# Row normalisation by the sum of absolute values: twelve-row tiles in four buffers, or sixteen-row tiles in three

## The chip, the cores and the metric

The kernel runs on one core of one Trainium2 chip. The metric is the device time of one execution in microseconds (us), the median of several runs. Before the change it is 316.64 us (three runs, 316.41 to 316.7).

## The reference

```python
batch, seq, dim = 32, 512, 1024
x = np.random.randn(batch, seq, dim).astype(np.float32)

def reference(x):
    sums = np.sum(np.abs(x), axis=-1, keepdims=True)
    return (x / (sums + 1e-8)).astype(np.float32)
```

There are 32 x 512 = 16,384 rows of 1,024 float32 values, 4 KB each. Every row is divided by the sum of its absolute values. The input is 67.1 MB and so is the output.

## The kernel before

The 16,384 rows are spread over the 128 partitions of the on-chip memory, 128 rows to a partition. A partition's rows of one tile lie side by side in DRAM, so that one partition of a tile is one run of consecutive bytes, up to 48 KB long.

There are eleven tiles: ten of 12 rows per partition (6 MB) and a last one of 8 (4 MB). The list `rows` holds these numbers. `piece` says where a tile lies in DRAM. Tiles 0, 1 and the last one share a block of 32 rows per partition (`HEAD`): their runs start 128 KB apart from partition to partition. Each of the other eight tiles is a block of its own, with runs 48 KB apart.

`load(i)` (L87) issues one transfer from DRAM into a buffer of the pool `sbuf`, which has four buffers of 12 rows (48 KB per partition each). It is issued on the queue of the SP engine. `max_dma_last_dim` limits the bytes that one DMA descriptor moves: tiles 0 and 1 are loaded in descriptors of 48 KB, the others in halves of 24 KB (16 KB for the last).

`normalize` does the arithmetic on a tile in place. On VectorE (DVE in the profile) it sums the absolute values of each row (L47), adds the small constant (L54) and takes the reciprocal (L56). Then it scales the rows, in up to three groups. The first `kv` rows are scaled by one multiplication with the broadcast reciprocals on VectorE (L58). The next `kt` rows are scaled one by one on VectorE (L65), and the rest one by one on ScalarE (ACT, L68). The table `split` gives the sizes of the last two groups for the first three tiles and the last two; the six tiles between them are scaled by L58 alone.

`store(i)` (L97) writes the tile back, on ACT's queue. Store 0 is cut into two transfers: three rows in descriptors of 4 KB, and nine rows in descriptors of 36 KB. The store of the last but two tiles is cut into two halves of six rows. The last two stores use 48 and 32 KB descriptors, the others 24 KB.

The order of work is written out by hand (`manual_schedule`). First come four loads. Then, for each tile: its arithmetic, its store, and the load of the tile four places further on, which reuses its buffer. That load therefore waits for this store to have landed. Each engine carries its instructions out in the order written; SP holds only loads, ACT holds its rows and all stores. The transfers of both queues are carried out by the same 16 DMA engines. A tile's 128 partitions are shared out evenly, eight to a DMA engine.

Of the kernel before, what the change touches and what calls it, by code (L numbers as in the profile page):

```python
# [1 line left out]

# [4 lines left out]

FP32 = mybir.dt.float32
EPS = 1e-8


@with_exitstack
def kernel(
    ctx: ExitStack,
    tc: tile.TileContext,
    x: bass.AP,
    out: bass.AP,
):
    nc = tc.nc
    P = nc.NUM_PARTITIONS  # L20

    x_flat = x.flatten_outer_dims()
    out_flat = out.flatten_outer_dims()
    n, d = x_flat.shape

    R = 12
    BUFS = 4
    HEAD = 32
    per_partition = n // P
    assert n % P == 0 and (per_partition - HEAD) % R == 0  # L30
    rows = [R] * ((per_partition - HEAD) // R + 2) + [HEAD - 2 * R]

    def piece(flat, i):
        head = flat[: P * HEAD, :].rearrange("(p r) d -> p r d", p=P)
        if i < 2:
            return head[:, R * i : R * (i + 1), :]
        if i == len(rows) - 1:
            return head[:, 2 * R :, :]
        a = P * (HEAD + R * (i - 2))
        return flat[a : a + P * R, :].rearrange("(p r) d -> p r d", p=P)  # L40

    sbuf = ctx.enter_context(tc.tile_pool(name="sbuf", bufs=BUFS))
    stats = ctx.enter_context(tc.tile_pool(name="stats", bufs=len(rows)))

    def normalize(x_tile, k, kv, kt):
        s = stats.tile([P, R], FP32)
        nc.vector.tensor_reduce(  # L47
            out=s[:, :k],
            in_=x_tile[:, :k, :],
            axis=mybir.AxisListType.X,  # L50
            op=mybir.AluOpType.add,
            apply_absolute_value=True,
        )
        nc.vector.tensor_scalar_add(out=s[:, :k], in0=s[:, :k], scalar1=EPS)  # L54
        inv = stats.tile([P, R], FP32)
        nc.vector.reciprocal(out=inv[:, :k], in_=s[:, :k])  # L56
        if kv:
            nc.vector.tensor_mul(  # L58
                out=x_tile[:, :kv, :],
                in0=x_tile[:, :kv, :],  # L60
                in1=inv[:, :kv].unsqueeze(2).to_broadcast([P, kv, d]),
            )
        for r in range(kv, kv + kt):
            row = x_tile[:, r, :]
            nc.vector.tensor_scalar_mul(out=row, in0=row, scalar1=inv[:, r : r + 1])  # L65
        for r in range(kv + kt, k):
            row = x_tile[:, r, :]
            nc.scalar.activation(  # L68
                out=row,
                in_=row,  # L70
                func=mybir.ActivationFunctionType.Copy,
                scale=inv[:, r : r + 1],
            )

    last = len(rows) - 1
    split = {0: (3, 4), 1: (0, 3), 2: (0, 3), last - 1: (0, 2), last: (4, 4)}

    tiles = {}

    HALF, WHOLE = 24576, 49152
    FIRST = 3

    def load(i):
        x_tile = tiles[i] = sbuf.tile([P, R, d], FP32, name="x_tile")
        nc.sync.dma_start(out=x_tile[:, : rows[i], :], in_=piece(x_flat, i), max_dma_last_dim=WHOLE if i < 2 else HALF)  # L87

    def store(i):
        if i == 0:  # L90
            parts = [(0, FIRST, 4 * d), (FIRST, R, WHOLE)]
        elif i == last - 2:
            parts = [(0, R // 2, HALF), (R // 2, R, HALF)]
        else:
            parts = [(0, rows[i], WHOLE if i >= last - 1 else HALF)]
        for a, b, size in parts:
            nc.scalar.dma_start(  # L97
                out=piece(out_flat, i)[:, a:b, :],
                in_=tiles[i][:, a:b, :],
                max_dma_last_dim=size,  # L100
            )

    def compute(i):
        k = rows[i]
        kt, ks = split.get(i, (0, 0))
        normalize(tiles[i], k, k - kt - ks, kt)

    with tc.manual_schedule():
        for i in range(BUFS):
            load(i)  # L110
        for i in range(len(rows)):
            compute(i)
            store(i)
            if i + BUFS < len(rows):
                load(i + BUFS)


# [1 line left out]
_INS = ['x']  # L119
_OUTS = [((32, 512, 1024), 'float32')]  # L120


# [23 lines left out]
```

## Time and profile before

The profiled execution has a span of 315.2 us; the median of the runs is 316.64 us.

| what | value |
|---|---|
| median of the runs | 316.64 us |
| span of the profiled execution | 315.2 us |
| first load issued, first reduce begins | 0.73, 17.80 us |
| last reduce begins, last store issued | 279.79, 293.25 us |
| VectorE busy | 260.6 us (83%) |
| of it L47, reduce (11 instructions) | 138.2 us |
| of it L58, multiply (10 instructions) | 113.6 us |
| of it L65, row by row (7 instructions) | 4.8 us |
| ACT busy | 18.5 us (6%) |
| L68, one row on ACT (16 instructions) | 1.138 us each |
| bytes moved, mean rate over the span | 134.22 MB, 426 GB/s |
| load of 6 MB, median from issue to landing | 36.9 us |

In the views of the profile, times are counted from the start of the span. q1 is the load queue (SP's), q10 the store queue (ACT's). In a view of windows the columns are: window, its length, busy time of VectorE, ACT and POOL with the number of instructions, the TensorE clock, the mean busy share of the 16 DMA engines, and GB/s. In a view of groups each line ends with busy time, mean length of one instruction in ns, and the idle time before them with what ended it. A packet is what a DMA engine carries out without a break; here, one descriptor.

### The profile page before, as it was taken

What the parts mean: (1) busy time and instruction counts of PE and PEld (TensorE: products, weight loads), DVE (VectorE), ACT (ScalarE), POOL (GpSimd) and SP (SyncE); (2) the same over time, 40 slices, a digit from 0 to 9 for tenths busy, and PEclk for the clock granted to TensorE, in tenths of its full rate; (3) what the DMA queues carried; (4) which work ended last, traced back from release to release, by engine and by line L of the source; (5) the groups of instructions that cost most, each with busy time, mean ns of one, the idle gap of its engine ahead of it and who ended that gap; (6) DMA issues with size and microseconds to landing.
All of it is one profiled execution on the core that took longest, in us unless ns stands there. A gap on an engine that the chain in (4) does not pass through costs nothing.

```text
span 315.2 us, 172 instructions
## 1 busy us (share of the span) xinstructions
DVE 260.6 (83%) x50; ACT 18.5 (6%) x17; POOL 0.2 (0%) x4
## 2 busy tenths in 40 slices
DVE  0079999999999999989996997999699969999000
ACT  0010503004000000000000000000000000203200
POOL 0000000000000000000000000000000000000000
DMA  8999999999999999999999999999999999999997
GB/s 318 480 399 412 437 407 464 411 436 413 415 446 437 415 446 437 415 449 434 415 449 437 412 449 437 412 449 437 415 446 437 415 437 434 432 428 496 399 408 324
DMA packets 5761, 134.22 MB, mean 426 GB/s; under 512 B 385, under 2 KB 385, under 8 KB 769
## 3 DMA queue, kind: packets, MB, share of 16 engines
q1 hardware_dynamic: 2736, 67.11, 49.8%
q10 hardware_dynamic: 3024, 67.11, 49.4%
q14 instruction: 1, 0.00, 0.0%
HBM read 67.11 MB, written 67.11 MB: 426 GB/s over the span
## 4 chain that ended last, share of the span: by engine, by line
DVE 40%; DMA 33%; another core or an unknown queue 18%; ACT 1%; issue 0%; SPq 0%
DVE s L47 23%; DMA x_tile<-in_x_dram 17%; DMA out_dram<-x_tile 16%; DVE x_tile L58 15%; ACT x_tile L68 1%; DVE x_tile L65 1%; DVE inv L56 0%; DVE s L54 0%; SPq L87 0%
## 5 line engine op out<-in xcount | busy, mean ns | idle before, releaser
L47 DVE TENSOR_REDUCE s<-x_tile 128x12 f32<-128x12288 f32 (+1 forms) x11 | 138.2, 12562 | 29.8 <-DMA x_tile<-in_x_dram 29.8
L58 DVE TENSOR_TENSOR x_tile<-x_tile,inv 128x12288 f32<-128x12288 f32 (+3 forms) x10 | 113.6, 11358 | 0.5
L68 ACT ACTIVATE x_tile<-x_tile,inv 128x1024 f32<-128x1024 f32 x16 | 17.2, 1138 | 256.9 <-DVE inv L56 256.9
L65 DVE TENSOR_SCALAR x_tile<-x_tile,inv 128x1024 f32<-128x1024 f32 x7 | 4.8, 749 | 0.0
L56 DVE RECIPROCAL inv<-s 128x12 f32<-128x12 f32 (+1 forms) x11 | 2.5, 226 | 0.4
L68 ACT ACT_TABLE_LOAD x1 | 1.3, 1283 | 17.8 <-DMA x_tile<-in_x_dram 17.8
L54 DVE TENSOR_SCALAR s<-s 128x12 f32<-128x12 f32 (+1 forms) x11 | 1.9, 174 | 0.4
L130 POOL MEMSET const-bfloat16-1.0<- 128x1 bf16 x1 | 0.1, 101 | 0.0
L130 POOL MEMSET const-uint8-127<- 128x1 uint8 x1 | 0.1, 101 | 0.0
L130 POOL MEMSET const-float32-0.0<- 128x1 f32 x1 | 0.1, 98 | 0.2 <-issue 0.2
L130 POOL MEMSET const-float32-1.0<- 128x1 f32 x1 | 0.1, 98 | 0.0
## 6 DMA issues: line engine op xcount, KB each, us to landing
x_tile<-in_x_dram SPq DMA_DIRECT2D x10, 6144.0 KB, 36.9
out_dram<-x_tile ACTq DMA_DIRECT2D x8, 6144.0 KB, 49.1
out_dram<-x_tile ACTq DMA_DIRECT2D x2, 3072.0 KB, 33.4
out_dram<-x_tile ACTq DMA_DIRECT2D x1, 4608.0 KB, 37.9
x_tile<-in_x_dram SPq DMA_DIRECT2D x1, 4096.0 KB, 32.2
out_dram<-x_tile ACTq DMA_DIRECT2D x1, 4096.0 KB, 20.9
out_dram<-x_tile ACTq DMA_DIRECT2D x1, 1536.0 KB, 29.3
```

Source lines behind the costliest of these rows:

```text
L47: nc.vector.tensor_reduce(out=s[:, :k], in_=x_tile[:, :k, :], axis=mybir.AxisListType.X, op=mybir.AluOpType.add, apply_absolute_value=True,)
L54: nc.vector.tensor_scalar_add(out=s[:, :k], in0=s[:, :k], scalar1=EPS)
L56: nc.vector.reciprocal(out=inv[:, :k], in_=s[:, :k])
L58: nc.vector.tensor_mul(out=x_tile[:, :kv, :], in0=x_tile[:, :kv, :], in1=inv[:, :kv].unsqueeze(2).to_broadcast([P, kv, d]),)
L65: nc.vector.tensor_scalar_mul(out=row, in0=row, scalar1=inv[:, r : r + 1])
L68: nc.scalar.activation(out=row, in_=row, func=mybir.ActivationFunctionType.Copy, scale=inv[:, r : r + 1],)
L130: nc = _bacc.Bacc("TRN2", target_bir_lowering=False, num_devices=1)
```

## The change

There are three buffers of 16 rows per partition in place of four of 12. The tiles are seven of 16 rows and two of 8 (`rows`), nine in all. They lie in three blocks (`pieces`): tiles 0 and 8 share 24 rows per partition, tiles 1 to 3 share 48, and tiles 4 to 7 share 56, so that the runs start 96, 192 and 224 KB apart.

`load` and `store` no longer limit the descriptors: one descriptor moves the whole run of a partition, 64 KB for a tile of 16 rows and 32 KB for a tile of 8. Each tile is stored by one transfer.

In `normalize` the multiplication with the broadcast reciprocals is gone. Every row is scaled by itself: the last three eighths of a tile's rows on ACT (6 of 16, 3 of 8), the others on VectorE (10 and 5). The reduce, the add and the reciprocal remain, on 16 or 8 rows. The table `split` and the cut stores go. The written order is as before, with three loads ahead, and with load i+3 after store i.

```diff
-    R = 12
-    BUFS = 4
-    HEAD = 32
-    per_partition = n // P
-    assert n % P == 0 and (per_partition - HEAD) % R == 0
-    rows = [R] * ((per_partition - HEAD) // R + 2) + [HEAD - 2 * R]
+    R = 16
+    BUFS = 3
+
+    pieces = [(0, 8), (1, 2, 3), (4, 5, 6, 7)]
+    rows = [16, 16, 16, 16, 16, 16, 16, 8, 8]
+    assert n == P * sum(rows)
+
+    place = {}
+    base = 0
+    for tiles_of in pieces:
+        per = sum(rows[i] for i in tiles_of)
+        at = 0
+        for i in tiles_of:
+            place[i] = (base, per, at)
+            at += rows[i]
+        base += P * per
 
     def piece(flat, i):
-        head = flat[: P * HEAD, :].rearrange("(p r) d -> p r d", p=P)
-        if i < 2:
-            return head[:, R * i : R * (i + 1), :]
-        if i == len(rows) - 1:
-            return head[:, 2 * R :, :]
-        a = P * (HEAD + R * (i - 2))
-        return flat[a : a + P * R, :].rearrange("(p r) d -> p r d", p=P)
+        start, per, at = place[i]
+        block = flat[start : start + P * per, :].rearrange("(p r) d -> p r d", p=P)
+        return block[:, at : at + rows[i], :]
...
-    def normalize(x_tile, k, kv, kt):
+    def normalize(x_tile, k, ks):
...
-        if kv:
-            nc.vector.tensor_mul(
-                out=x_tile[:, :kv, :],
-                in0=x_tile[:, :kv, :],
-                in1=inv[:, :kv].unsqueeze(2).to_broadcast([P, kv, d]),
-            )
-        for r in range(kv, kv + kt):
+        for r in range(k - ks):
             row = x_tile[:, r, :]
             nc.vector.tensor_scalar_mul(out=row, in0=row, scalar1=inv[:, r : r + 1])
-        for r in range(kv + kt, k):
+        for r in range(k - ks, k):
             row = x_tile[:, r, :]
             nc.scalar.activation(
...
-    split = {0: (3, 4), 1: (0, 3), 2: (0, 3), last - 1: (0, 2), last: (4, 4)}
...
-        nc.sync.dma_start(out=x_tile[:, : rows[i], :], in_=piece(x_flat, i), max_dma_last_dim=WHOLE if i < 2 else HALF)
+        nc.sync.dma_start(out=x_tile[:, : rows[i], :], in_=piece(x_flat, i))
 
     def store(i):
-        if i == 0:
-            parts = [(0, FIRST, 4 * d), (FIRST, R, WHOLE)]
-        elif i == last - 2:
-            parts = [(0, R // 2, HALF), (R // 2, R, HALF)]
-        else:
-            parts = [(0, rows[i], WHOLE if i >= last - 1 else HALF)]
-        for a, b, size in parts:
-            nc.scalar.dma_start(
-                out=piece(out_flat, i)[:, a:b, :],
-                in_=tiles[i][:, a:b, :],
-                max_dma_last_dim=size,
-            )
+        nc.scalar.dma_start(out=piece(out_flat, i), in_=tiles[i][:, : rows[i], :])
...
-            compute(i)
+            normalize(tiles[i], rows[i], 3 * rows[i] // 8)
             store(i)
             if i + BUFS < len(rows):
                 load(i + BUFS)
```

More of the change, by code (lines that the diff above doesn't have):

```diff
@@ L24 @@
     n, d = x_flat.shape
-    R = 12
-    BUFS = 4
-    HEAD = 32
-    per_partition = n // P
-    assert n % P == 0 and (per_partition - HEAD) % R == 0
-    rows = [R] * ((per_partition - HEAD) // R + 2) + [HEAD - 2 * R]
-    def piece(flat, i):
-        head = flat[: P * HEAD, :].rearrange("(p r) d -> p r d", p=P)
-        if i < 2:
-            return head[:, R * i : R * (i + 1), :]
-        if i == len(rows) - 1:
-            return head[:, 2 * R :, :]
-        a = P * (HEAD + R * (i - 2))
-        return flat[a : a + P * R, :].rearrange("(p r) d -> p r d", p=P)
+    R = 16
[12 more added lines that the diff above has]
+        base += P * per
+    def piece(flat, i):
+        start, per, at = place[i]
+        block = flat[start : start + P * per, :].rearrange("(p r) d -> p r d", p=P)
+        return block[:, at : at + rows[i], :]
     sbuf = ctx.enter_context(tc.tile_pool(name="sbuf", bufs=BUFS))
-    stats = ctx.enter_context(tc.tile_pool(name="stats", bufs=len(rows)))
-    def normalize(x_tile, k, kv, kt):
+    stats = ctx.enter_context(tc.tile_pool(name="stats", bufs=2 * len(rows)))
+    def normalize(x_tile, k, ks):
         s = stats.tile([P, R], FP32)
@@ L73, in normalize @@
             )
-    last = len(rows) - 1
-    split = {0: (3, 4), 1: (0, 3), 2: (0, 3), last - 1: (0, 2), last: (4, 4)}
     tiles = {}
-    HALF, WHOLE = 24576, 49152
-    FIRST = 3
     def load(i):
         x_tile = tiles[i] = sbuf.tile([P, R, d], FP32, name="x_tile")
-        nc.sync.dma_start(out=x_tile[:, : rows[i], :], in_=piece(x_flat, i), max_dma_last_dim=WHOLE if i < 2 else HALF)
+        nc.sync.dma_start(out=x_tile[:, : rows[i], :], in_=piece(x_flat, i))
     def store(i):
-        if i == 0:
-            parts = [(0, FIRST, 4 * d), (FIRST, R, WHOLE)]
-        elif i == last - 2:
-            parts = [(0, R // 2, HALF), (R // 2, R, HALF)]
-        else:
-            parts = [(0, rows[i], WHOLE if i >= last - 1 else HALF)]
-        for a, b, size in parts:
-            nc.scalar.dma_start(
-                out=piece(out_flat, i)[:, a:b, :],
-                in_=tiles[i][:, a:b, :],
-                max_dma_last_dim=size,
-            )
[L103 to L106, printed above, removed]
+        nc.scalar.dma_start(out=piece(out_flat, i), in_=tiles[i][:, : rows[i], :])
     with tc.manual_schedule():
```

## The prediction

> **What bounds the kernel now.** I read the page's slices and queues first, to see which resource has no gaps.
>
> ```profile
> span 315.2 us, 172 instructions
> ...
> DVE 260.6 (83%) x50; ACT 18.5 (6%) x17; POOL 0.2 (0%) x4
> ...
> DMA  8999999999999999999999999999999999999997
> ...
> DMA packets 5761, 134.22 MB, mean 426 GB/s; under 512 B 385, under 2 KB 385, under 8 KB 769
> ...
> q1 hardware_dynamic: 2736, 67.11, 49.8%
> q10 hardware_dynamic: 3024, 67.11, 49.4%
> ```
>
> The packets of the load queue (q1, issued by SP) and of the store queue (q10, issued by ACT) fill 49.8% + 49.4% = 99.2% of the 16 DMA engines' span: 312.7 of 315.2 us. Only the first and last slices are below 9 tenths. VectorE has 54.6 us to spare. So the kernel is bound by bytes, which don't change, and a new version can gain only what packets cost beside their bytes. It can lose any stretch in which both queues are empty.
>
> Next come the loads' waits, the windows, and the instructions by form.
>
> ```profile
> SPq L87 <- DMA out_dram<-x_tile: 242.1, 8, 63.3
> ```
> ```profile
> 12.00:14.00 2.00, 0.00 (x0) 0.00 (x0) 0.00 (x0) 1.00 0.91 393
> 292.00:294.00 2.00, 0.00 (x0) 1.22 (x2) 0.00 (x0) 1.00 0.91 393
> ```
> ```profile
> L47 DVE TENSOR_REDUCE s<-x_tile 128x12 f32<-128x12288 f32 x10 | 129.5, 12949 | 29.8 <-DMA x_tile<-in_x_dram 29.8
> ...
> L47 DVE TENSOR_REDUCE s<-x_tile 128x8 f32<-128x8192 f32 x1 | 8.7, 8686 | 0.0
> ```
> ```profile
> 0.73 247.25 SPq L87 DMA_DIRECT2D x_tile<-in_x_dram  x11
> 17.80 12.95 DVE L47 TENSOR_REDUCE s<-x_tile 128x12 f32<-128x12288 f32 x1 [17.80 <-DMA x_tile<-in_x_dram]
> ...
> 36.67 2.07 DVE L65 TENSOR_SCALAR x_tile<-x_tile,inv 128x1024 f32<-128x1024 f32 x3
> 36.78 2.40 ACTq L97 DMA_DIRECT2D out_dram<-x_tile  x2
> ...
> 288.96 4.27 ACT L68 ACTIVATE x_tile<-x_tile,inv 128x1024 f32<-128x1024 f32 x4 [17.82 <-DVE inv L56]
> 288.96 2.74 DVE L65 TENSOR_SCALAR x_tile<-x_tile,inv 128x1024 f32<-128x1024 f32 x4
> 293.25 0.34 ACTq L97 DMA_DIRECT2D out_dram<-x_tile  x1
> ```
>
> Every load past the fourth waits for a store to land, for its buffer. In each window shown 16 packets of 48 KB start, one per engine: 0.91 x 2.00 us = 1.82 us each. The last store is issued at 293.25, while the store before it still runs (issued 279.85, landed 304.5 by its semaphore), so the engines have work to the end.
>
> **Descriptors.** The trace's packet records give the spacing of packets on one engine: 1.812 us for 48 KB, 1.209 for 32 KB, 0.908 for 24 KB. The slope from 24 to 48 KB is 0.904 us / 24,576 B = 0.0368 ns per byte, which leaves 4 to 5 ns per packet. A 64 KB packet, of which the trace has none, is then an estimated 2.414 us; were its fixed part ten times larger it would be 2.45. Now each engine moves (5761 - 385) / 16 = 336 data packets; after it is 2 x (7 x 8 + 2 x 8) = 144. So 192 x 4.5 ns = **0.9 us less**. Beside it, load packets followed by a store packet are 6.5 ns longer than the rest on average (914.8 against 908.3 ns, 1,637 of them), nearly all of it between 39 and 65 us, where the 4 KB pieces of store 0 alternate with load packets: 0.66 us per engine. This can go with those pieces (0.66) or come back where stores first meet loads (0); I take 0.3, the middle.
>
> **Compute.** The reduce grows by (12.949 - 8.686) / 4 = 1.066 us a row: 17.2 us for 16 rows. The add and the reciprocal take 0.5 us (30.77 to 31.26). The multiply at L58 goes; its rows move to L65, at 2.07 / 3 to 2.74 / 4 = 0.69 us each on VectorE (10 of 16, 5 of 8), and to ACT at 4.27 / 4 = 1.07 us (6 and 3). So 17.2 + 0.5 + 6.9 = 24.6 us for a 16-row tile and 8.7 + 0.5 + 3.4 = 12.6 for an 8-row one; ACT's 6.4 and 3.2 run beside VectorE's. VectorE's sum falls to 7 x 24.6 + 2 x 12.6 = 197 us. This is worth **nothing** by itself: the transfers of a 16-row tile take 16 x 2.414 = 38.6 us and cover it. The nine loads and nine stores, for eleven and thirteen, cost no path time either, at about 0.4 us of queue time each, under running transfers. On ACT the store of a tile stands before the next tile's rows, which aren't due for another 17 us; on SP only loads stand behind a waiting load. POOL has no part in it.
>
> **First tile.** Load 0 now lands at 17.78 after eight packets, so 3.3 us are start. It will land at 3.3 + 8 x 2.414 = 22.6, and store 0 is issued at 47.3. Loads 1 and 2 keep the engines busy to 3.3 + 24 x 2.414 = 61.2. Cost 0.
>
> **Three buffers.** Load i+3 now waits for store i. Store 0 lands when 32 packets have gone, 3.3 + 32 x 2.414 = 80.5, and store 1 was issued some 9 us before, at about 71.7. In the middle each cycle has 38.6 us of transfers against 24.6 + about 2 for issue and landing, so about 12 us of cover: a store is always queued when the next load is issued. Cost 0 there; if the cover went, the missing time would be paid once a cycle.
>
> **The tail** decides. Load 8 waits for store 5. Before that the engines must do loads 0 to 6 and stores 0 to 5, 104 packets: 3.3 + 251.1 = 254.4; load 7's eight 32 KB packets alternate with store 5's, so it lands between 254.4 and 264.1. All but store 8 is done at 3.3 + 112 x 2.414 + 24 x 1.209 = 302.7. Store 8 is to be ready by then. It needs load 8 landed (0.4), 12.7 us of compute and 1.0 us from issue to first packet (load 0: issued 0.73, first packet 1.74), so load 8 must land by 289.0. If load 8 is issued at 264.1 and alternates one for one with all of store 6, it lands at about 264.1 + 1.0 + 8 x (2.414 + 1.209) = 294.1, less one packet if it goes first: 291.7. The engines then stand idle for 2.7 to 5.1 us. Each packet of store 6 that doesn't get in front takes off 2.4 us; two packets decide.
>
> What settles the order is how a new transfer gets in. In the trace a transfer that comes to busy engines starts late: store 0, issued at 36.78, has its first packet at 40.54, 3.75 us after; load 4, issued at 76.84, at 80.45, 3.6 after. That is 2.6 us more than on idle engines, and on most engines three 24 KB packets start in between. Read as packets already taken from the other queue, it is three of 64 KB, 7.2 us; read as time it stays 2.6 us, one packet. I take the count, because the 2.6 us are close to three packets in both places, though equal sizes can't prove it. Then the loads, newcomers in each cycle, fall behind the stores, so that store 5 lands at about 261, load 8 joins behind load 7 with no wait of its own, and store 6, issued at 262 to 267, is the newcomer. Load 8, with its first packet near 263, then has one to six store packets in between: it lands at 276 to 288.3 (263 + 9.7 + 0.4 and 2.4 for each). **Cost 0**; the bounds of the tail are 0 and 5.1 + 2.6 = 7.7 us.
>
> **Sum.** Span 315.2 - 0.9 - 0.3 = 314.0. The median of the runs is 316.64 - 315.16 = 1.5 above the profiled span, so **315.4 us**, a gain of 0.4%. The walk's own end, 302.7 + 8 x 1.209 + 0.4 + 1.0 = 313.8, agrees.
>
> **A rule that speaks against the change.** The trace's packets alternate one for one between the queues wherever both have work. The Trainium skill's page "DMA: Bandwidth & Descriptors", section "Queues, rings and completion order", says that an engine drains a whole packet of typically 9 to 17 descriptors from one queue before it switches. The rival on whole transfers below is worked out as a mechanism of this kernel.
>
> **The rivals.**
> - *The newcomer's delay is a time, and the tail starves.* Load 8 comes after 289 us, and the engines wait for store 8. For it: the delay is the same 3.6 to 3.75 us twice; the walk without a count of packets is 3 to 5 us too late. Against it: packets taken ahead explain the same rows. Price 2 to 7.7, say 4.4: 319.8 us, **slower**; it decides once load 8 lands after 289.
> - *Engines drain one queue's whole share of a transfer before they switch.* Store 6's eight packets go first, 264 to 283.3; load 8 ends at 293.0, lands at 293.4, store 8's first packet is at 307.1, 4.4 us late: 319.8. Against it: alternation by single packets in all mixed stretches of the trace.
> - *The large descriptor doesn't arrive as one packet but as two of 32 KB.* Then 256 packets per engine, 0.5 us of the 0.9 given back, and a newcomer's three packets are again small, 3.6 us: idle 0 to 2. 315.9 to 317.9, say 316.5.
> - *The new strides cost rate.* Partition runs now start 96, 192 and 224 KB apart, for 48 and 128 KB. Against it: 48 KB packets took 1.815 us at both old strides. 1% of the transfers is 3 us: 318.4.
>
> **How the numbers follow.** Chances: covered tail 45%, delay as a time 36%, two packets 9%, strides 6%, whole transfers 4%. A difference under 0.2%, 0.63 us, can't be told from none in this kernel. Of the covered tail I put 38 of 45 below 316.0, the rest within; two packets is 1 faster, 5 within, 3 slower; the delay as a time is 2 within and 34 slower; the other two are slower. Faster 39%, same 14%, slower 47%. The forecast's own range is 314.7 to 316.3. With the starved tail it reaches to 320.8, where the top of its bound and the far strides are left out.
>
> **What would show it.** Right: q1 and q10 together at 99% of a span near 314; packets of 64 KB at 2.41 us; all slices but the outer ones at 9; the last reduce starting by 289; VectorE busy near 197. Wrong: a gap in the DMA row in slices 38 to 40, the last reduce after 289, with the gap as long as the reduce is late; or packets well above 2.41 us; or 32 KB packets throughout. A gap in the middle of the span would show that three buffers fail in the cycle, which nothing above expects.

## The result, and the profile after

The changed kernel takes **328.82 us** (median of four runs, 327.32 to 330.79) against 316.56 for the kernel before on the same chips (316.41 to 316.7): a ratio of 1.0391, 95% interval 1.0352 to 1.0429. The profiled execution is the fastest of the four, 327.32 us, with a span of 325.54 us (315.16 before). So 10.4 of the 12.3 us are in the profile, whose run is 1.5 us faster than the median. About 0.15 us lie outside the span: 1.78 us here, for 1.63 in 47 later runs of the kernel before. A run more than 1.5% above the fastest of its kernel counts as slow and stays out of the medians and ranges below, which concerns one run of experiment 3 (321.85 us) and one of experiment 7 (330.01 us).

The page of the changed kernel, span, slices and queues:

```profile
span 325.5 us, 256 instructions
...
DVE 195.4 (60%) x107; ACT 52.2 (16%) x49; POOL 0.2 (0%) x4
...
DMA  9899898989999999998998999999999998989647
...
DMA packets 2594, 134.24 MB, mean 412 GB/s; under 512 B 288, under 2 KB 288, under 8 KB 288
...
q1 hardware_dynamic: 1296, 67.11, 48.4%
q10 hardware_dynamic: 1296, 67.11, 48.0%
```

The two queues fill 96.4% of the span, where they filled 99.2%: by the packet records 313.7 us of packets on each engine, for 312.9 before. The bytes take about as long as they did; what is new is time without packets. The DMA row shows where: a 6 and a 4 in the slices 38 and 39. VectorE's time fell by a quarter, and the kernel is slower all the same.

The same stretch in the view of windows (window, length, busy time of VectorE, ACT and POOL, clock, DMA share, GB/s), and in the timeline (start, length, engine, line):

```profile
264.00:266.00 2.00, 1.06 (x2) 0.64 (x1) 0.00 (x0) 1.00 0.19 82
...
306.00:308.00 2.00, 2.00 (x1) 0.00 (x0) 0.00 (x0) 1.00 0.12 49
308.00:314.00 6.00, 5.29 (x8) 3.23 (x3) 0.00 (x0) 1.00 0.00 0
```
```profile
240.53 17.22 DVE L53 TENSOR_REDUCE s<-x_tile 128x16 f32<-128x16384 f32 x1 [14.24 <-DMA x_tile<-in_x_dram]
...
265.15 0.34 ACTq L82 DMA_DIRECT2D out_dram<-x_tile  x1
267.83 8.69 DVE L53 TENSOR_REDUCE s<-x_tile 128x8 f32<-128x8192 f32 x1 [2.77 <-DMA x_tile<-in_x_dram]
...
280.54 0.34 ACTq L82 DMA_DIRECT2D out_dram<-x_tile  x1
300.83 8.69 DVE L53 TENSOR_REDUCE s<-x_tile 128x8 f32<-128x8192 f32 x1 [20.37 <-DMA x_tile<-in_x_dram]
...
313.54 0.34 ACTq L82 DMA_DIRECT2D out_dram<-x_tile  x1
```

The chain that ended last has store 5 and load 8 in these two pieces (start, length):

```profile
226.38 40.22 DMA out_dram<-x_tile
...
266.67 34.13 DMA x_tile<-in_x_dram
```

The last tile is reduced from 300.83, after VectorE has waited 20.37 us for load 8. Its store is issued at 313.54; the engines ran out of other work near 306.3. That is the large hole, 7.9 us by the packet records (16 engines' mean, 306.2 to 314.5). A small one of 1.2 us lies at 264.4 to 266.2: on 13 of the engines load 7 and store 5 are done, store 6 is only issued at 265.15, and load 8 waits until 266.67 for store 5 to land. Before there was no hole at all between the first packet and the last. 7.9 + 1.2 us of holes and 0.8 us more of packets are 9.9 of the 10.4 us; the rest lies at the start, at the end and in the few ns by which the record of one packet overlaps the next.

### The profile page after: what moved, and what is told of

Same layout as the page of the kernel before. It is cut to its first block, busy times and chain, and to the rows that moved or that the text cites. A ratio compares the mean times of both kernels' runs of the same rounds, so it can differ in the third digit from the quotient of the medians.

```text
span 325.5 us, 256 instructions
## 1 busy us (share of the span) xinstructions
DVE 195.4 (60%) x107; ACT 52.2 (16%) x49; POOL 0.2 (0%) x4
## 2 busy tenths in 40 slices
DMA packets 2594, 134.24 MB, mean 412 GB/s; under 512 B 288, under 2 KB 288, under 8 KB 288
## 4 chain that ended last, share of the span: by engine, by line
DMA 57%; DVE 26%; another core or an unknown queue 12%; issue 0%; DVEq 0%; SPq 0%; ACTq 0%
DMA x_tile<-in_x_dram 31%; DMA out_dram<-x_tile 27%; DVE s L53 19%; DVE x_tile L65 7%; DVE inv L62 0%; DVE s L60 0%; DVEq L117 0%; SPq L79 0%; DVEq L65 0%; ACTq L82 0%
## 5 line engine op out<-in xcount | busy, mean ns | idle before, releaser
L53 DVE TENSOR_REDUCE s<-x_tile 128x16 f32<-128x16384 f32 (+1 forms) x9 | 137.9, 15323 | 116.8 <-DMA x_tile<-in_x_dram 116.8
L68 ACT ACTIVATE x_tile<-x_tile,inv 128x1024 f32<-128x1024 f32 x48 | 50.9, 1137 | 238.2 <-DVE inv L62 238.2
L65 DVE TENSOR_SCALAR x_tile<-x_tile,inv 128x1024 f32<-128x1024 f32 x80 | 53.8, 749 | 0.7
L62 DVE RECIPROCAL inv<-s 128x16 f32<-128x16 f32 (+1 forms) x9 | 2.2, 242 | 0.3
L60 DVE TENSOR_SCALAR s<-s 128x16 f32<-128x16 f32 (+1 forms) x9 | 1.6, 174 | 0.3
```

Source lines behind the costliest of these rows:

```text
L53: nc.vector.tensor_reduce(out=s[:, :k], in_=x_tile[:, :k, :], axis=mybir.AxisListType.X, op=mybir.AluOpType.add, apply_absolute_value=True,)
L68: nc.scalar.activation(out=row, in_=row, func=mybir.ActivationFunctionType.Copy, scale=inv[:, r : r + 1],)
```

## The experiments

Each is compared with the kernel before, run beside it (316.58 or 316.59 us median in these sets). "A" to "D" in the expectations are the theories as they were put there.

**1 and 2. Descriptors of 32 and of 16 KB** in the changed kernel.

```diff
-        nc.sync.dma_start(out=x_tile[:, : rows[i], :], in_=piece(x_flat, i))
+        nc.sync.dma_start(out=x_tile[:, : rows[i], :], in_=piece(x_flat, i), max_dma_last_dim=32768)
...
-        nc.scalar.dma_start(out=piece(out_flat, i), in_=tiles[i][:, : rows[i], :])
+        nc.scalar.dma_start(out=piece(out_flat, i), in_=tiles[i][:, : rows[i], :], max_dma_last_dim=32768)
```

> The changed kernel with one thing undone: each run of a partition moves in descriptors of at most 32 KB (two per partition for 16 rows). Theory A, packet size: in the changed kernel a transfer's completion waits for one more packet of the other queue (last packet of load 3 ends at 121.0, its reduce begins at 123.8), engines fall a packet out of step, and a newcomer waits for packet boundaries, all priced in packets of 2.42 us. With 1.21 us packets load 8 then lands by about 290 in place of 300.8, and the gap before the last store shrinks from 8 us to 0 to 2: 315.5 to 318 us. Theory B, three buffers: load 8 can't be issued before store 5 has landed near 265, whatever the packets; the gap stays at 6 to 8 us: 325 to 329. Theory C, strides: packets lose rate through the 96 to 224 KB strides; unchanged too, 327 to 329.

> The changed kernel with descriptors of at most 16 KB. Theory A: the three packet costs halve again, but 576 packets per engine at 4.8 ns cost 2 us more than 144 do: 316 to 318.5, gap near 0. Theory B: as the changed kernel, 325 to 331. Theory C: 327 to 331.

Measured: 320.77 us (320.1 to 321.17) and 321.32 us (320.6 to 321.83), ratios 1.0129 (1.0112 to 1.0146) and 1.0149 (1.013 to 1.0167). Both are 2.8 us above what theory A allowed and far below B and C. (With 16 KB there are 512 packets per engine, not 576; they take 315.7 us, 2 us more than the changed kernel's.) Page and timeline with 32 KB:

```profile
DMA  8999999999999999999999999999999997999997
```
```profile
266.40 8.68 DVE L53 TENSOR_REDUCE s<-x_tile 128x8 f32<-128x8192 f32 x1
266.58 0.38 ACTq L82 DMA_DIRECT2D out_dram<-x_tile  x1
...
287.97 8.69 DVE L53 TENSOR_REDUCE s<-x_tile 128x8 f32<-128x8192 f32 x1 [8.95 <-DMA x_tile<-in_x_dram]
300.69 0.35 ACTq L82 DMA_DIRECT2D out_dram<-x_tile  x1
```

The large hole is gone: the last reduce begins at 287.97, inside the prediction's limit of 289. The small one has stayed and grown, 2.4 us at 264.8 to 267.7 (the 7 in slice 34), so it doesn't come from the size of the packets alone. Besides it, packets are longer than their size asks by 3.2 us per engine, for 1.4 in the kernel before; 2.4 + 1.8 us are about what separates it from the kernel before, 4.2 us. With 16 KB the last reduce begins at 291.45 and the small hole is 1.7 us.

**3. The kernel before with 48 KB descriptors** in place of 24.

```diff
-    HALF, WHOLE = 24576, 49152
+    HALF, WHOLE = 49152, 49152
```

> The kernel before with all its 24 KB descriptors made 48 KB and nothing else. Theory A: each completion waits 1.8 us in place of 0.9, but four buffers and a tail of which the last load is issued near 247 leave slack: no gap, and 100 fewer packets per engine save 0.5 us: 316 to 317.5. If large packets cost by themselves (a stall per packet or a lower rate), 320 or more. Theory B: 316 to 316.6.

Measured: 318.65 us over nine runs, ratio 1.0046 (1.0021 to 1.007): 2 us slower, between the two ranges that were expected (316 to 317.5 and 320 or more). The runs scatter from 316.13 to 319.52, while those of the kernel before stay within 316.41 and 316.85 in all sets. The windows at the end of its profiled execution:

```profile
300.00:308.00 8.00, 0.00 (x0) 0.00 (x0) 0.00 (x0) 1.00 0.86 373
308.00:312.00 4.00, 0.00 (x0) 0.00 (x0) 0.00 (x0) 1.00 1.16 500
312.00:314.00 2.00, 0.00 (x0) 0.00 (x0) 0.00 (x0) 1.00 0.08 33
314.00:316.00 2.00, 0.00 (x0) 0.00 (x0) 0.00 (x0) 1.00 0.04 16
```

(Windows count a packet whole where it starts.) No hole, but the 16 engines don't end together: between 312.85 and the last packet a mean of 2.6 us is lost, for 0.3 us before. Here engines are a large packet or two out of step.

**4. A tail of 12 and 4 rows** in the changed kernel, with its 64 KB descriptors.

```diff
-    rows = [16, 16, 16, 16, 16, 16, 16, 8, 8]
+    rows = [16, 16, 16, 16, 16, 16, 16, 12, 4]
```

> The changed kernel with its last two tiles of 12 and 4 rows in place of 8 and 8; 64 KB descriptors and three buffers stay. If the loss is the gap in the tail (theories A and B alike), the last tile's own load and compute fall from 9.7 + 12.6 to 4.8 + 6.9 us and the store before it grows by 4.8: gap 0 to 2, 317 to 320 us. If the loss is rate or stalls spread over the span (theory C), 325 to 329.

Measured: 319.64 us (318.43 to 320.76), ratio 1.0097 (1.006 to 1.0133). Its DMA row has no hole, and both tiles of the tail come in time:

```profile
DMA  9999999999999999999999999999999999999995
```
```profile
273.81 12.95 DVE L53 TENSOR_REDUCE s<-x_tile 128x12 f32<-128x12288 f32 x1 [7.83 <-DMA x_tile<-in_x_dram]
292.80 0.34 ACTq L82 DMA_DIRECT2D out_dram<-x_tile  x1
296.40 4.42 DVE L53 TENSOR_REDUCE s<-x_tile 128x4 f32<-128x4096 f32 x1 [3.69 <-DMA x_tile<-in_x_dram]
303.50 0.34 ACTq L82 DMA_DIRECT2D out_dram<-x_tile  x1
```

So with everything else of the change in place, the shape of the tail alone is worth 9 us.

**5. Only store 6 in 32 KB descriptors.**

```diff
+        nc.scalar.dma_start(out=piece(out_flat, i), in_=tiles[i][:, : rows[i], :], max_dma_last_dim=32768 if i == 6 else 65536)
```

> The changed kernel; store 6 alone moves in two 32 KB descriptors per partition, all else in 64 KB. Theory D, turns: the queues take turns by packets, so load 8's eight 32 KB packets each wait for one 64 KB packet of store 6 (8 x 3.63 = 29 us), and that is what makes the last reduce late. With equal packets load 8 takes 8 x 2.42 = 19.4 us, the last reduce begins near 291 in place of 300.8, and the gap of 8 us falls to 0 to 1: 319 to 322 us. Theory A as first put (completions and steps between engines, in all transfers): those are unchanged but for one transfer, so the gap stays at 5 us or more: 325 or more.

Measured: 321.13 us (319.27 to 322.86), ratio 1.0143 (1.0088 to 1.0197). Page and timeline:

```profile
DMA  9999999999999999999999999999999999899997
```
```profile
268.12 8.69 DVE L53 TENSOR_REDUCE s<-x_tile 128x8 f32<-128x8192 f32 x1 [2.65 <-DMA x_tile<-in_x_dram]
280.83 0.35 ACTq L82 DMA_DIRECT2D out_dram<-x_tile  x1
292.63 8.69 DVE L53 TENSOR_REDUCE s<-x_tile 128x8 f32<-128x8192 f32 x1 [11.88 <-DMA x_tile<-in_x_dram]
305.35 0.34 ACTq L82 DMA_DIRECT2D out_dram<-x_tile  x1
```

One transfer, which load 8 neither waits for nor follows, brings the last reduce from 300.83 to 292.63 and the time down by 7.7 us. The large hole is gone; the small one, 1.5 us, stays. By the packet records load 8's data takes 19.6 us (271.4 to 291.1) in place of 27.6 (271.6 to 299.2), which is the whole gain. Theory D holds: load 8 pays for the length of the packets with which it takes turns.

**6. The tail of 12 and 4 rows with 32 KB descriptors.** Both edits from above.

> The changed kernel with both the 12 and 4 row tail and 32 KB descriptors. If the two defects are separate, an 8 us gap by turns in the tail and a 2.4 us gap near 265 where the short load 7 leaves the engines without work before store 6 comes, both are gone: 316 to 318 us, no gap over 0.5. If three buffers cost by themselves in every cycle (theory B), 319 or more.

Measured: 317.37 us over ten runs (317.13 to 317.89), ratio 1.0028 (1.0018 to 1.0037).

```profile
span 315.4 us, 256 instructions
...
DMA  8999999999999999999999999999999999999997
```

No hole is left, with three buffers, tiles of 16 rows, the new blocks and rows scaled one by one. Three buffers cost nothing that can be seen in the cycle.

**7. Every tile a block of its own,** so that the runs start 64 KB apart.

```diff
-    pieces = [(0, 8), (1, 2, 3), (4, 5, 6, 7)]
+    pieces = [(i,) for i in range(9)]
```

> The changed kernel with every tile a block of its own: a partition's runs start 64 KB apart (32 KB for the last two) in place of 96, 192 and 224 KB. Theory C, strides matter: the packets' mean length changes by more than 1% and the time by 3 us or more, either way. Otherwise the time is that of the changed kernel, 327 to 331, with packets of 2.418 us.

Measured: 329.21 us over three runs (325.09 to 329.49), ratio 1.0358 (1.0289 to 1.0428), the changed kernel's own time within the scatter of both. The trace is that of the run at 330.01 us. Its data packets take 313.6 us per engine, for 313.5 in the changed kernel, and a 64 KB packet 2.418 us in both. Strides of 64 to 224 KB make no difference here.

**8. Rows scaled one by one in the kernel before.**

```diff
-        kt, ks = split.get(i, (0, 0))
+        ks = 3 * k // 8
+        kt = k - ks
```

> The kernel before with the broadcast multiply replaced by rows one by one on two engines (8 and 4 of 12, 5 and 3 of 8), nothing else. If the transfers cover the compute, as predicted, 316.3 to 317 us with VectorE near 190 us busy; if stores that are issued 3 to 5 us earlier matter, up to 1 us less or more.

Measured: 317.43 us over ten runs (317.17 to 317.61), ratio 1.0026 (1.0017 to 1.0035). VectorE is busy 199.7 us in place of 260.6, and the kernel is 0.85 us slower: over the first range given and inside the second (up to 1 us either way). About 0.15 us of it lie outside the span (1.78 us for 1.63, with 277 instructions for 172); where the other 0.7 come from wasn't settled.

**9. The last load of the kernel before in 8 KB descriptors,** the turns tested in the other kernel and the other way round.

```diff
-max_dma_last_dim=WHOLE if i < 2 else HALF)
+max_dma_last_dim=WHOLE if i < 2 else 8192 if i == last else HALF)
```

> The kernel before; its last load alone moves in 8 KB descriptors (32 packets per engine in place of 16 of 16 KB), nothing else. Theory D, turns by packets: from 255 us each of its packets waits for one store packet. 27 turns go against the 24 KB packets of the stores still queued (27 x 1.21 = 32.8 us, to 288) and five against 48 KB ones (5 x 2.12 = 10.6), so it lands near 298 to 299 in place of 279.8, the last store is issued near 312 in place of 293.3, and the engines stand idle for some 9 us from 304: 323 to 327 us. If an engine shares by bytes or by time, or drains a queue, the load lands as before and the time is 316.5 to 317.

Measured: 322.26 us (322.17 to 322.44), ratio 1.018 (1.0166 to 1.0194), 0.7 us below the range of theory D. Page and timeline:

```profile
DMA  8999999999999999999999999999999999999647
```
```profile
295.16 8.69 DVE L47 TENSOR_REDUCE s<-x_tile 128x8 f32<-128x8192 f32 x1 [15.49 <-DMA x_tile<-in_x_dram]
308.62 0.34 ACTq L97 DMA_DIRECT2D out_dram<-x_tile  x1
```

Halving the packets of one load makes it land late enough that the last reduce begins 15.4 us later (295.16, for 279.79), and puts the changed kernel's hole into the kernel before: 5.8 us, from 303.6 to 309.6. The walk had it 3 us later still.

**10. Store 0 of the kernel before in one transfer** of 24 KB descriptors.

```diff
-            parts = [(0, FIRST, 4 * d), (FIRST, R, WHOLE)]
+            parts = [(0, R, HALF)]
```

> The kernel before with store 0 as one transfer in 24 KB descriptors, without the three rows in 4 KB pieces. The step of the prediction that gave 0.3 (0 to 0.66) us to these pieces: if their stall goes with them, 315.9 to 316.3; if it comes back where stores first meet loads (in the changed kernel it did, 1.2 us between 48 and 52), 316.4 to 317, with store 0 landing later than 76.8.

Measured: 317.04 us over eleven runs (316.84 to 317.5), ratio 1.0016 (1.0007 to 1.0025): slower by 0.46 us. Of these 0.34 lie outside the span (1.98 us, for 1.64 in the kernel before beside it). The packets between 40 and 60 us are 0.77 us per engine longer than their size asks; in the kernel before this was 0.56 us at 62 to 64. Over the whole execution it is 1.4 us in both: the stall came back, and nothing was won.

None of the ten beats the kernel before.

## Why the prediction was wrong

**The step that failed** is the one in the tail that began "What settles the order is how a new transfer gets in" and ended "I take the count". It read the 2.6 us by which a newcomer was late as three packets already taken, hence 7.2 us with 64 KB, and from that followed stores ahead of loads, load 8 landing by 276 to 288.3 and a cost of 0. The delay is a time. From the packet records, from issue to first packet, with the engines busy on the other queue:

| packets in the engines | issue to first packet, us |
|---|---|
| 16 KB (experiment 2) | 3.6 to 4.0 |
| 24 KB (before) | 3.6, 3.75 |
| 32 KB (experiment 1) | 3.5, 4.1 |
| 48 KB (experiment 3) | 3.7, 4.5 |
| 64 KB (after: load 3, store 0) | 3.5, 4.3 |

By the count, on top of the 1.0 us of idle engines, the first row would be some 2.8 us (1.0 + 3 x 0.61) and the last over 8 (1.0 + 7.2). So the rival "the newcomer's delay is a time, and the tail starves" was the case, and its deciding point, load 8 after 289 us, was passed by 12 us. The sign named for it came too, a gap in slices 38 to 40, but the gap is 7.9 us and not as long as the reduce is late, because the engines' other work ended at 306.3 and not at 302.7. The prediction's own chances held slower (47%) likelier than faster (39%); the forecast went with the likeliest single case. Its bounds for load 8, 276 to 288.3, come to 275.5 to 287.6 by its own terms; nothing hangs on this.

**The size.** That rival was priced 2 to 7.7 us, at 319.8 us. Its walk had load 8 issued at 264.1 at the latest and landing at 291.7 to 294.1; it was issued at 266.67 and landed at 300.80. Against the 294.1, the issue was 2.57 us late, the entry took 3.95 us more, the data 1.37 us less, and the completion, which this walk left out, 1.57 us: 6.72 us in all. Term by term:
- *Completions.* A transfer's landing was taken 0.4 us after its last packet. The trace has a packet of 4 bytes at the end of each engine's share of a transfer, and it takes its turn like any other: with the other queue busy, loads land 0.97 us after their last data packet with 16 KB packets, 1.27 with 24 KB, 1.6 with 32 KB and 2.8 with 64 KB; with it empty 0.35. That is 0.35 plus one packet of the other queue (0.61, 0.91, 1.21, 2.42). The Trainium skill's page "DMA: Bandwidth & Descriptors", section "Why a DMA increments its semaphore by 16 and not by 1", says that each engine's last descriptor is the write to the semaphore, which lands only after that engine's data. The trace agrees: the 4-byte packet stands last on each engine, and it takes a turn as well. Store 5's last data packet ended at 265.05, and SP's wait for it at 266.6.
- *Entry.* I had given load 8 1.0 us from issue to first packet, as on idle engines. Store 6 had just come in on 13 of them, and it took 5.0.
- *Turns.* The eight turns of 3.6 us were in the walk, and were right: load 8's packets start 3.6 us apart on each engine while store 6 lasts, the first at 271.6, and the last ends at 299.2. Experiments 5 and 9 show them directly, one made better and one worse by nothing but packet sizes.

The hole at 264 wasn't in the sum at all. I had named about 12 us of cover in each cycle, from 38.6 us of transfers. In the cycle of load 7 the transfers are only 8 x (2.42 + 1.21) = 29 us, and load 6's 24.6 us of compute, landing and issue no longer fit. Experiments 4 and 6, with 12 rows there, have no such hole.

**The rest, step by step.** *Descriptors:* a 64 KB packet takes 2.418 us (2.414 estimated), and there are 144 per engine; the fixed part saved is 0.9 us, as said. But packets were also stretched by 3.9 us per engine over what their size asks, in place of 1.4: 0.6 and 0.7 at the start, 1.2 between 48 and 52, where store 0 meets the loads, and 1.6 from 266 to 298. So the 0.3 us for the 4 KB pieces was wrong in sign for this change: the stretch where stores first meet loads grew. In experiment 10, without these pieces, it came back as well. *Compute:* a 16-row tile takes 17.2 + 0.5 + 6.7 us and VectorE 195.4 us in all (24.6 and 197 predicted); that this is worth nothing was nearly right: nothing was won, and experiment 8 is 0.85 us slower. *First tile:* reduced from 22.75 (22.6). *Three buffers:* no hole in the cycle (experiment 6). *Two packets for one* was not the case: 2594 packets less 288 of 4 bytes and 2 of an instruction queue are 2,304, 144 per engine. *Strides* were excluded by experiment 7, and *whole transfers at a time* by 5 and 9: the queues take turns by single packets, here single descriptors, as load 8's spacing of 3.6 us (2.42 + 1.21) shows. The Trainium skill's page "DMA: Bandwidth & Descriptors", section "Queues, rings and completion order", speaks of packets of typically 9 to 17 descriptors between switches. These traces don't agree with it.

**What the change costs, in parts.** From 328.8 us, equal packets against load 8 bring 321.1 (experiment 5), the other tail 319.6 (4), the other tail and 32 KB descriptors everywhere 317.4 (6). What is left to 316.6, 0.8 us, is about the 0.85 us by which rows scaled one by one slow the kernel before (8); that the two are the same thing wasn't shown.

## What to carry to other kernels

Where DMA engines are full, look for the last load that waits for a store, and walk from there to the last store: entry (3.5 to 5 us here on busy engines), turns, completion, compute; all of that must fit under the transfers that are still queued. Queues that take turns by packets share an engine in proportion to their packet sizes (experiments 5 and 9), so a load that must be quick should not take turns with a store of larger packets. Cutting descriptors from 64 to 32 KB cost an estimated 0.5 us here (112 more packets per engine at 4 to 5 ns) and won 8 us (experiment 1).

## What the runs showed of the hardware

- The delay of a newcomer whose own queue is empty is 3.4 to 4.6 us on engines busy with the other queue, at five packet sizes from 16 to 64 KB, and 0.84 to 1.1 us on idle ones. What happens in the 2.5 us and more between wasn't found.
- A completion waits for one packet of the other queue, 0.6 to 2.4 us.
- Runs with large packets scatter more: 316.13 to 319.52 us with 48 KB in the kernel before, 316.41 to 316.85 with 24 KB; 318.43 to 320.76 with 64 KB and 317.13 to 317.89 with 32 KB in the tail of 12 and 4 rows.
- In each profiled execution, around the entry of an early store, the 16 engines lose 0.4 to 1.2 us on average with packets that take longer than their size asks (62 us before, 48 to 52 after). It moved with the stores and didn't vanish in any kernel. Those with the hole near 264 lose another 1.0 to 1.5 us between 266 and 276, when the next load and store come in. The cause of both stays open.
